# RWKV streams in three stages (front, inverse, chain), with TensorE's order written out in rounds

## The chip, the cores and the metric

One core of one Trainium2 chip runs the whole program in one launch. The metric is device time in microseconds, the median of several executions. The core has five engines with a queue each: TensorE (PE, matmuls and transposes; its weight loads are listed as PEld), VectorE (DVE), ScalarE (ACT), GpSimd (POOL) and SyncE (SP, which here issues the DMAs).

## The reference

Two layers of a hybrid backbone over 1024 latent tokens and 256 context tokens, width 1024. Layer 0 is RWKV-7 time mixing beside a Mamba-2 branch, layer 1 an mLSTM beside attention. The change touches only the RWKV branch, a delta rule that is run in both directions, first over the context and then, with the state left there, over the latent tokens:

```python
    def step(S, inp):
        r_t, k_t, v_t, w_t, a_t, kk_t = inp
        Skk = jnp.einsum('dbhvk,dbhk->dbhv', S, kk_t)
        S = S * w_t[..., None, :] - Skk[..., :, None] * (kk_t * a_t)[..., None, :] + v_t[..., :, None] * k_t[..., None, :]
        return S, jnp.einsum('dbhvk,dbhk->dbhv', S, r_t)
...
    w_pre = p['w0'] + jnp.einsum('btdr,drc->btdc', jnp.tanh(wl), p['w2'])
    decay = jnp.exp(-jnp.exp(-jax.nn.softplus(-w_pre) - 0.5))
    a = jax.nn.sigmoid(p['a0'] + jnp.einsum('btdr,drc->btdc', al, p['a2']))
    kk = hs(k * p['k_k'])
    kk = kk / jnp.maximum(jnp.sqrt(jnp.sum(kk * kk, -1, keepdims=True)), 1e-12)
    k_dir = k[:, :, None] * (1.0 + (a - 1.0) * p['k_a'])
    y, S_fin = rwkv7_bidir_scan(hs(r), hs(k_dir), hs(v), hs(decay), hs(a), kk, S0)
    # group norm of y per head, plus a bonus term, times the branch's gate
```

There are 8 heads of 64 columns: four blocks `ct` of 128 columns, two heads each. Everything is float32.

## The kernel before

The kernel cuts the 1280 tokens into chunks of 64 and works through them in closed form. A *unit* is two chunks (NG = 2) of one block of 128 columns in both directions, which makes four products `j` (two chunks, two directions) of two heads each; a block has NU = 10 units, the first two of them the context. Two streams run side by side: stream 0 does the blocks 0 and 1, stream 1 the blocks 2 and 3, 20 units each.

The parts, all generators whose `yield` marks the end of a step:

- `rwkv_prep(st, ct)`, once per block: five pieces of 256 tokens, four steps each. It loads r, k, v and the low-rank input `al` (single buffers, tags `pr`, `pk`, `pv`, `pal`), and in the same first step multiplies `al` with `a2`; then normalises kk (line 612 and following, with a square root on ScalarE and a reciprocal on VectorE), forms the bonus and turns v; results go to DRAM (`kk_d`, `bv_d`, `vt_d`).
- `rwkv_unit(st, ct, gi)`: first the *front*: loads of `wa`, r, k, kk and of v into SV, two matrix products into PSUM (tag `mm`), four tanh (line 686), the decay's running sum (`tensor_tensor_scan`), three exponentials, and the products AR, KB and RZ (lines 708 to 714). Then the *inverse*: the product MN (evacuated in line 730), transposes KT, MT and TT, and the inverse of a unit triangular matrix by doubling: an identity turn and five levels b = 2, 4, ..., 32. Each level has an X turn (evacuated by a masked multiplication into Xs, line 783), a T turn into Tm (lines 809, 816) and a TT turn into TT (line 817); a turn is 16 matmuls of 64x64 in two or four quadrants of the array. The PSUM tile `rec0` or `rec1` of a stream has one buffer of two banks, so a turn waits for the evacuation of the turn before.
- `rwkv_chain(st, ct, gi)`: the sequential part over the unit's two chunks: four short steps per chunk (pw, pu, pS, py) in the one-bank PSUM tile `ch0` or `ch1`, which carry the state in SV and write y (line 879).
- `rwkv_finish(st, ct)`, once per block: the norm over y, five turns and the gate (lines 887 to 916), which uses the tags `pr`, `pk`, `pv` of the preparation again.

`rwkv_stream` puts them in order. It runs `pace(unit q+1, chain q)`, which takes a step of the chain with every other step of the unit, and every third time a step of the side work (the next block's preparation from unit 4 on, the last block's finish). All side work goes through `alone`, a lock that one generator holds from its start to its end across both streams. At a block's unit 8 the stream stops until its side work is done; at a block's unit 0 it lets the unit run and holds the chain back while side work is left. `lockstep` takes one step of each stream in turn.

While the streams begin, `mix` puts in the part of the output projection that needs no RWKV result (`out_part`: two column halves, ten token tiles each, 24 matmuls per tile into PSUM `oa`, evacuated in line 1262), one step for `mix3` = 3.0 lock steps; when it is done the streams run on alone (`run(r)`). The rest of the projection (`out_gemm`) follows the streams.

The order of the instructions on each engine is made when the program is built: a planner takes the instruction that its own costs say is ready first, and the order in which the code issues them decides between several. Inside `tc.manual_schedule(engines={PE})` TensorE's instructions stay instead in the order in which the code issues them. The Mamba stage and the attention already stand in such a block; the RWKV stage does not. Every engine works its queue in that fixed order, and an instruction whose input is not there holds up what is behind it.

Of the kernel before, what the change touches and what calls it, by code (L numbers as in the profile page):

```python
# [149 lines left out]
class K:  # L150
    mix0 = 2.2
    mix2 = 1.25
    mix1 = 0.5
    mix3 = 3.0
    mixa = 0.6
# [396 lines left out]
    def rwkv_setup(s, rp):  # L552
# [18 lines left out]
        s.tt, s.wa, s.rz, s.mt = {}, {}, {}, {}  # L571
        for st in range(2):
            for i in range(2):
                s.tt[st, i] = rp.tile([128, 2 * NG, 64], F32, name=f"TT{st}{i}")
                s.wa[st, i] = rp.tile([128, 2, 2, 64 * NG], F32, name=f"wa{st}{i}")
                s.rz[st, i] = rp.tile([128, 2 * NG, 2, 64], F32, name=f"RZ{st}{i}")
                nc.gpsimd.memset(s.wa[st, i], 0.0)
                nc.gpsimd.memset(s.rz[st, i], 0.0)
            s.mt[st] = rp.tile([128, 2 * NG, 64], F32, name=f"MT{st}")
# [64 lines left out]

    def rwkv_unit(s, st, ct, gi):

# [15 lines left out]
        r, k, kk = tl("ur", [64]), tl("uk", [64]), tl("ukk", [64])  # L662
        par = s.tn[st] % 2
        s.tn[st] += 1
        wa = s.wa[st, par]
        TT, RZ, MT = s.tt[st, par], s.rz[st, par], s.mt[st]
        SV = X["sv", gi] = tl("SV", [2, 2, 64], 2)
        for d in range(2):
            for j in range(2):
                s.load(wa[H[d], j, d], s.u_rk[12 + j][H[d], sl[d]])  # L670
        for d in range(2):
            for x, src in ((r, s.u_rk[ct]), (k, s.u_rk[4 + ct]), (kk, s.kk_d[ct])):
                s.load(flat(x)[:, L * d:L * d + L], src[:, sl[d]])
        for d in range(2):
            vsrc = s.vt_d[ct][:, NG * gs[d]:NG * gs[d] + NG]
            for h in range(2):
                for q in range(2):
                    s.load(SV[H[1 - h], NG * d:NG * d + NG, q, h], vsrc[H[1 - h]])
        pp = s.psum("mm", (128, 2, 2, L))
        for j, w in ((0, s.w2), (1, s.a2)):  # L680
# [12 lines left out]
        for d in range(2):  # L693
# [4 lines left out]
            nc.vector.tensor_tensor_scan(v(P), sm[:, ::-1] if d else sm, v(sg), 0.0, ALU.mult, ALU.add)  # L698
        E2 = tl("E2", [64], 2)
        nc.vector.tensor_sub(sg, P, sg)  # L700
# [12 lines left out]
        for h in range(2):  # L713
            nc.gpsimd.tensor_mul(RZ[H[h], :, h], E2[H[h]], r[H[h]])

        def kb(j, h):

            return KB[H[h], j, 1 - h:3 - h].rearrange("p a b -> p (a b)")

        yield  # L720
        MN = tl("MN", [2, 2, 64], 2)
# [68 lines left out]

        Tm = tl("Tm", [64], 2)
        own = {(j, h): (h, j) for j in range(NJ) for h in range(2)}
# [5 lines left out]
        for n, b in enumerate((2, 4, 8, 16, 32)):  # L798
            px = pt_()
            iX = turn(MT, own, Tm, iT, side[n], area(px, 0), (lambda j: j // 2) if n else None)  # L800
            Xs = tl("Xs", [64])
            mask(Xs, area(px, 0), f"l{b}", n > 0)
            yield
            pz = pt_()
            if b < 32:
                iT = turn(TT, iTT, Xs, iX, (), area(pz, 0), (lambda j: j // 2) if n else None)
            if n == 0:
                Tm = tl("Tm", [64], 2)
                nc.scalar.copy(Tm.rearrange("p (b s) l -> p b (s l)", b=2), area(pz, 0))
                pt = pt_()  # L810
            else:
                pt = pz
            iTT = turn(Xs, iX, TT, iTT, side[n + 1], area(pt, 1), (lambda j: j % 2) if 0 < n < 4 else (lambda j: j // 2))
            if n and b < 32:
                Tm = tl("Tm", [64], 2)
                nc.scalar.copy(Tm.rearrange("p (b s) l -> p b (s l)", b=2), area(pz, 0))
            nc.scalar.copy(TT.rearrange("p (b s) l -> p b (s l)", b=2), area(pt, 1))
            yield
# [109 lines left out]
    def rwkv_stream(s, st, cts):  # L928

        seq = [(ct, gi) for ct in cts for gi in range(s.NU)]  # L930
        yield from s.alone(s.rwkv_prep(st, cts[0]))
        yield from s.rwkv_unit(st, *seq[0])
        side = []
# [3 lines left out]

        for q, (ct, gi) in enumerate(seq):
            if gi == 4 and ct != cts[-1]:
                side.append(s.alone(s.rwkv_prep(st, cts[cts.index(ct) + 1])))  # L940
            u = s.rwkv_unit(st, *seq[q + 1]) if q + 1 < len(seq) else iter(())
            while side and gi == 0:
                side = more()
                next(u, None)
                yield
            for i, _ in enumerate(pace(u, s.rwkv_chain(st, ct, gi))):
                if i % 3 == 2:
                    side = more()
                yield
            if gi == s.NU - 2:  # L950
                while side:
                    side = more()
                    yield
            if gi == s.NU - 1:
                side.append(s.alone(s.rwkv_finish(st, ct)))
        while side:
# [342 lines left out]
    def layer0(s):  # L1299
# [45 lines left out]
        oa = s.pool("oa")  # L1345
        mix(r, s.out_part(oa, 0, "wabo", range(4, 12), y0, range(10), s.xin, xa, "oa", 1, 1), s.mix3, lambda: True)
        oa.release()
        ob = s.pool("ob")
        s.load_gates(0, ob)
        W = s.out_weights(ob, ob, "wabo", range(4))  # L1350
        run(r)
        rp.release()
# [732 lines left out]
```

## Time and profile before

| | |
|---|---|
| median of 3 runs | 3806.43 us (3802.72 to 3806.52) |
| the profiled execution | 3797.94 us, span 3796.1 us |
| TensorE busy in the span | 3366.2 us (89%), 29178 matmuls |
| VectorE, ScalarE, GpSimd busy | 2208.6 (58%), 1493.0 (39%), 1116.6 us (29%) |
| mean granted TensorE clock | 0.92 |
| RWKV stage, 865 to 1925 us | 1060 us, TensorE busy 862.5, VectorE 616.2, ScalarE 482.6, clock 0.82 |

A row of the view by stretches gives the stretch and its length, then each engine's busy time with the number of its instructions (a query for one line or tile lists only the engines that it concerns), then the granted TensorE clock as a share of full speed, the share of the DMA engines' time, and GB/s. A row of the timeline gives start, duration, engine, line, operation, output and inputs by the program's tile names, tile shape, how many instructions were merged, and in brackets the engine's idle time before it with what ended it. Matmuls are pipelined and their ends are modelled, so a group's duration is longer than the time after which the next group may start.

### The profile page before, as it was taken

The page shows a single profiled execution, that of the slowest core. Times are in us where ns is not written, and L with a number is a line of the kernel's source. Part 1 is how long each engine was busy: PE and PEld are TensorE (multiplying, and loading weights), DVE is VectorE, ACT ScalarE, POOL GpSimd, SP SyncE. Part 2 cuts the span into 40 slices and gives each one's busy share as a digit, 9 for nine tenths or more (in the row PEclk, how much of TensorE's full clock was granted, in tenths as well). Part 3 has the DMA queues.
Part 4 walks back from the last instruction along what each step waited for, and adds up shares of the span by engine and source line. Part 5 has one row for each costly group of instructions (what it writes and reads, how often), then busy time and mean ns, then how long its engine had stood idle before and what let it go on. Part 6 is the DMA issues. An engine that isn't in the chain of part 4 may idle for free. (4 is left out here: it accounts for less than half of the span.)

```text
span 3796.1 us, 74040 instructions
## 1 busy us (share of the span) xinstructions
PE 3366.2 (89%) x29178; PEld 2650.6 (70%) x29178; DVE 2208.6 (58%) x4053; ACT 1493.0 (39%) x3219; POOL 1116.6 (29%) x1071
## 2 busy tenths in 40 slices
PE   7999998996888888789769899999999788999978
PEld 3687776773566666577557798788888566666757
DVE  3576487773566666466557705433443488777645
ACT  3232233333434545444433322322332225666751
POOL 0112276662333221222102112112222255444330
PEclk9999998896898978699779999999999899999989
DMA  6526444435543222221133332654554451000023
GB/s 237 180 75 199 137 166 155 157 124 181 149 127 98 69 71 67 75 56 47 36 106 101 120 95 85 190 180 139 161 163 143 138 165 53 23 23 22 19 81 111
DMA packets 394276, 429.58 MB, mean 113 GB/s; under 512 B 81376, under 2 KB 317760, under 8 KB 391368
## 3 DMA queue, kind: packets, MB, share of 16 engines
q1 hardware_dynamic: 393928, 424.83, 35.7%
q8 instruction: 231, 3.78, 0.4%
q14 instruction: 117, 0.96, 0.1%
HBM read 306.62 MB, written 118.05 MB: 112 GB/s over the span
## 5 line engine op out<-in xcount | busy, mean ns | idle before, releaser
L211 PE MATMUL mm<-hh,wh 128*128 128x512 f32 (+1 forms) x1640 | 634.7, 387 | 0.0
L211 PE MATMUL mm<-hh,wl 128*128 128x512 f32 (+1 forms) x1640 | 610.6, 372 | 0.6 <-POOL wl L358 0.6
L211 PE MATMUL mm<-hl,wh 128*128 128x512 f32 (+1 forms) x1640 | 608.7, 371 | 0.0
L358 POOL TENSOR_TENSOR wl<-wr,wh 128x1024 fp32r<-128x1024 f32 x99 | 249.3, 2522 | 544.2 <-ACT wh L357 500.7
L211 PEld LDWEIGHTS mm<-hh,wh 128*128 128x128 f32 x1640 | 315.0, 192 | 66.0 <-issue 12.2
L211 PEld LDWEIGHTS mm<-hl,wh 128*128 128x128 f32 x1640 | 314.2, 192 | 61.7 <-issue 10.4
L211 PEld LDWEIGHTS mm<-hh,wl 128*128 128x128 f32 x1640 | 313.5, 191 | 59.5 <-issue 3.4
L1830 POOL TENSOR_SCALAR aP<-aP,adn,one 128x1280 f32<-128x1280 f32 x128 | 192.5, 1504 | 282.0 <-DVE adn L1829 146.4
L211 PE MATMUL mm<-wh,hh 128*128 128x256 f32 x736 | 216.3, 294 | 0.0
L1823 DVE TENSOR_REDUCE amx<-sc 128x1 f32<-128x1024 f32 x128 | 156.0, 1219 | 100.5 <-PE sc L211 100.3
L211 PE MATMUL mm<-wl,hh 128*128 128x256 f32 x736 | 208.3, 283 | 2.7 <-POOL wl L358 1.8
L211 PE MATMUL mm<-wh,hl 128*128 128x256 f32 x736 | 207.6, 282 | 0.0
L214 PE MATMUL tp<-mk,aP 128*128 128x128 f32 x1280 | 181.0, 278 | 5.0 <-ACT aPT L1838 5.0
L1838 ACT COPY aPT<-tp 128x512 f32<-128x512 f32 x256 | 145.5, 588 | 80.6 <-PE tp L214 78.9
L211 PE MATMUL pv<-aPT,aV 128*64 128x256 f32 x1280 | 168.1, 393 | 0.0
L214 PEld LDWEIGHTS tp<-mk,aP 128*128 128x128 f32 x1280 | 142.5, 141 | 35.9 <-issue 20.4
L357 ACT CAST wh<-wr 128x1024 fp32r<-128x1024 f32 x99 | 103.3, 1046 | 154.4 <-PE mm L211 128.4
L211 PE MATMUL sc<-akT,aqs 128*128 128x512 f32 x512 | 153.3, 422 | 1.7 <-DVE aqs L1808 1.1
L1111 POOL TENSOR_SCALAR sel<-mk,mdfd,mdt 128x128 f32<-128x128 f32 x160 | 128.9, 821 | 74.3 <-DVE E L1135 56.7
L211 PE MATMUL oa<-wh,yh 128*128 128x512 f32 x288 | 128.7, 447 | 24.3 <-DVE o L1262 11.9
L783 DVE TENSOR_TENSOR Xs<-rec,mk 128x256 f32<-128x256 f32 x200 | 83.6, 422 | 103.7 <-PE rec L211 101.5
L211 PEld LDWEIGHTS mm<-wl,hh 128*128 128x128 f32 x736 | 139.9, 190 | 3.7 <-POOL wl L358 2.5
(423 smaller groups left out, 7881.3 us busy)
## 6 DMA issues: line engine op xcount, KB each, us to landing
wr<-in_wcd SPq DMA_DIRECT2D x60, 512.0 KB, 5.3
adaw<-in_ada SPq DMA_DIRECT2D x48, 512.0 KB, 5.2
R<-rowd SPq DMA_DIRECT2D x20, 1024.0 KB, 5.6
wr<-in_wab SPq DMA_DIRECT2D x38, 512.0 KB, 4.1
yr<-y SPq DMA_DIRECT2D x36, 512.0 KB, 3.7
xt<-xtok SPq DMA_DIRECT2D x20, 512.0 KB, 5.0
SV<-vtd SPq DMA_DIRECT2D x320, 32.0 KB, 2.2
lva<-lv SPq DMA_DIRECT2D x19, 514.0 KB, 5.5
```

What stands on the lines that cost most here:

```text
L211: return s.nc.tensor.matmul(out, lhsT, rhs, start=start, stop=stop)
L214: return s.nc.tensor.transpose(out, in_, ident)
L357: nc.scalar.copy(hi, raw)
L358: nc.gpsimd.tensor_sub(lo, raw, hi.bitcast(F32))
L783: nc.vector.tensor_mul(half(t), out.rearrange("p b (s l) -> p b s l", s=2), m_)
L1111: nc.gpsimd.tensor_scalar(sel[:, h], s.m("slt"), s.dfd[:, o:o + 1], dtb[:, h:h + 1], ALU.mult, ALU.add)
L1823: nc.vector.tensor_reduce(mx[:, 1:2], ps, AX.X, ALU.max)
L1830: nc.gpsimd.tensor_scalar(P, P, dn[:, 3:4], s.one, ALU.mult, ALU.mult)
L1838: copy(out, pp.rearrange("p (a b) q -> p a (b q)", a=out.shape[1]))
```

## The change

`rwkv_unit` is split: its front becomes the generator `rwkv_front`, which runs one unit further ahead, with its two products in PSUM tag `oa` in place of `mm`; what it hands on gets one more buffer (E2 and RZ three). SV's loads move to the start of the inverse. `rwkv_stream` runs rounds: in each, the inverse of unit q+1, the front of unit q+2 and the chain of unit q, a step of the inverse first, a lock step's end, then a step of the chain, in some iterations one of the front, in every other iteration one of the side work. Only the first preparation of each stream takes the lock. The next block's preparation starts at unit 1 (stream 0) or 4 (stream 1) and has to be done by unit 3 or 6; during a finish the chain of the next block's unit 0 is held back. Both loops of the stage stand in `manual_schedule` for TensorE, and `mix3` becomes 2.0. Tm gets one buffer for two, and there is one more yield inside the first level.

```diff
@@ class K
-    mix3 = 3.0
+    mix3 = 2.0
@@ rwkv_setup
         for st in range(2):
+            for i in range(3):
+                s.rz[st, i] = rp.tile([128, 2 * NG, 2, 64], F32, name=f"RZ{st}{i}")
+                nc.gpsimd.memset(s.rz[st, i], 0.0)
             for i in range(2):
...
-                s.rz[st, i] = rp.tile([128, 2 * NG, 2, 64], F32, name=f"RZ{st}{i}")
-                nc.gpsimd.memset(s.rz[st, i], 0.0)
@@
-    def rwkv_unit(s, st, ct, gi):
+    def rwkv_front(s, st, ct, gi):
...
-        par = s.tn[st] % 2
+        n = s.tn[st]
         s.tn[st] += 1
-        wa = s.wa[st, par]
-        TT, RZ, MT = s.tt[st, par], s.rz[st, par], s.mt[st]
-        SV = X["sv", gi] = tl("SV", [2, 2, 64], 2)
+        wa, RZ = s.wa[st, n % 2], s.rz[st, n % 3]
...
-        for d in range(2):
-            vsrc = s.vt_d[ct][:, NG * gs[d]:NG * gs[d] + NG]
-            for h in range(2):
-                for q in range(2):
-                    s.load(SV[H[1 - h], NG * d:NG * d + NG, q, h], vsrc[H[1 - h]])
-        pp = s.psum("mm", (128, 2, 2, L))
+        yield
+        pp = s.psum("oa", (128, 2, 2, L))
...
-        E2 = tl("E2", [64], 2)
+        E2 = tl("E2", [64], 3)
...
+        X["f", gi] = AR, KB, E2, RZ, n
+
+    def rwkv_unit(s, st, ct, gi):
...
+        AR, KB, E2, RZ, n = X.pop(("f", gi))
+        TT, MT = s.tt[st, n % 2], s.mt[st]
...
+        SV = X["sv", gi] = tl("SV", [2, 2, 64], 2)
+        for d in range(2):
+            g = NG * s.og(d, gi)
+            vsrc = s.vt_d[ct][:, g:g + NG]
+            for h in range(2):
+                for q in range(2):
+                    s.load(SV[H[1 - h], NG * d:NG * d + NG, q, h], vsrc[H[1 - h]])
...
-        yield
         MN = tl("MN", [2, 2, 64], 2)
...
-        Tm = tl("Tm", [64], 2)
+        Tm = tl("Tm", [64])
...
             if n == 0:
-                Tm = tl("Tm", [64], 2)
+                Tm = tl("Tm", [64])
                 nc.scalar.copy(Tm.rearrange("p (b s) l -> p b (s l)", b=2), area(pz, 0))
+                yield
                 pt = pt_()
@@ rwkv_stream
-        yield from s.alone(s.rwkv_prep(st, cts[0]))
-        yield from s.rwkv_unit(st, *seq[0])
...
-        for q, (ct, gi) in enumerate(seq):
-            if gi == 4 and ct != cts[-1]:
-                side.append(s.alone(s.rwkv_prep(st, cts[cts.index(ct) + 1])))
-            u = s.rwkv_unit(st, *seq[q + 1]) if q + 1 < len(seq) else iter(())
-            while side and gi == 0:
-                side = more()
-                next(u, None)
+        def part(fn, q):
+            return fn(st, *seq[q]) if 0 <= q < len(seq) else None
+
+        def step(g):
+            return g if g is not None and next(g, 0) is None else None
+
+        for _ in s.alone(s.rwkv_prep(st, cts[0])):
+            yield
+        for _ in s.rwkv_front(st, *seq[0]):
+            yield
+            yield
+        for q in range(-1, len(seq)):
+            gi = seq[q][1] if q >= 0 else -1
+            if q >= 0 and gi == 1 + 3 * st and seq[q][0] != cts[-1]:
+                side.append(s.rwkv_prep(st, cts[cts.index(seq[q][0]) + 1]))
+            u, f, c = part(s.rwkv_unit, q + 1), part(s.rwkv_front, q + 2), part(s.rwkv_chain, q)
+            i = 0
+            while u or f or c or (side and gi == 3 + 3 * st):
+                u = step(u)
                 yield
-            for i, _ in enumerate(pace(u, s.rwkv_chain(st, ct, gi))):
-                if i % 3 == 2:
+                if not (side and gi == 0):
+                    c = step(c)
+                if i % 2 == 0 and i != 2:
+                    f = step(f)
+                if i % 2 or gi == 0:
                     side = more()
+                i += 1
                 yield
-            if gi == s.NU - 2:
-                while side:
-                    side = more()
-                    yield
             if gi == s.NU - 1:
-                side.append(s.alone(s.rwkv_finish(st, ct)))
+                side.append(s.rwkv_finish(st, seq[q][0]))
@@ layer0
-        mix(r, s.out_part(oa, 0, "wabo", range(4, 12), y0, range(10), s.xin, xa, "oa", 1, 1), s.mix3, lambda: True)
+        with s.tc.manual_schedule(engines={mybir.EngineType.PE}):
+            mix(r, s.out_part(oa, 0, "wabo", range(4, 12), y0, range(10), s.xin, xa, "oa", 1, 1), s.mix3, lambda: True)
...
-        run(r)
+        with s.tc.manual_schedule(engines={mybir.EngineType.PE}):
+            run(r)
```

More of the change, by code (lines that the diff above doesn't have):

```diff
@@ L714, in rwkv_unit, with tl @@
             nc.gpsimd.tensor_mul(RZ[H[h], :, h], E2[H[h]], r[H[h]])
+        X["f", gi] = AR, KB, E2, RZ, n
+    def rwkv_unit(s, st, ct, gi):
+        nc, rp = s.nc, s.rp
+        X = s.RX[ct]
+        NJ = 2 * NG
+        H = [slice(0, 64), slice(64, 128)]
+        AR, KB, E2, RZ, n = X.pop(("f", gi))
+        TT, MT = s.tt[st, n % 2], s.mt[st]
+        def tl(nm, w, bufs=1):
+            return rp.tile([128, NJ] + list(w), F32, tag=f"{nm}{st}", name=s.name(nm), bufs=bufs)
+        SV = X["sv", gi] = tl("SV", [2, 2, 64], 2)
[5 more added lines that the diff above has]
+                    s.load(SV[H[1 - h], NG * d:NG * d + NG, q, h], vsrc[H[1 - h]])
         def kb(j, h):
             return KB[H[h], j, 1 - h:3 - h].rearrange("p a b -> p (a b)")
-        yield
         MN = tl("MN", [2, 2, 64], 2)
@@ L814, in rwkv_unit @@
             if n and b < 32:
-                Tm = tl("Tm", [64], 2)
+                Tm = tl("Tm", [64])
                 nc.scalar.copy(Tm.rearrange("p (b s) l -> p b (s l)", b=2), area(pz, 0))
```

## The prediction

> **What bounds the kernel now.** I read the page first, then busy time by stretches, then the counts of single source lines in the same stretches, then the timeline.
>
> ```profile
> span 3796.1 us, 74040 instructions
> PE   7999998996888888789769899999999788999978
> PEclk9999998896898978699779999999999899999989
> ```
>
> One slice is 94.9 us. The RWKV stage is slices 10 to 20; there TensorE's busy digit is 7 to 9 and its clock digit falls to 6, while slices 21 to 31 stand at 9 and 9. The stage runs from 865 us (first matmul of the output projection's part) to 1925 us (last store of the second finish):
>
> ```profile
> core 0: us, PE busy (x) PEld busy (x) DVE busy (x) ACT busy (x) POOL busy (x), PEclk, DMA share, GB/s
> 865.00:1045.00 180.00, 139.47 (x737) 88.76 (x737) 80.31 (x131) 74.29 (x130) 53.09 (x53) 0.76 0.55 166
> 1211.00:1495.00 284.00, 246.09 (x5190) 193.41 (x5190) 192.38 (x431) 153.77 (x433) 65.90 (x85) 0.84 0.26 70
> 1495.00:1621.00 126.00, 90.98 (x1502) 67.10 (x1498) 66.80 (x142) 57.68 (x149) 28.10 (x36) 0.69 0.25 72
> 1621.00:1852.00 231.00, 208.24 (x5145) 167.94 (x5146) 148.69 (x362) 109.64 (x361) 51.33 (x69) 0.95 0.18 46
> 1893.00:1925.00 32.00, 5.83 (x21) 3.19 (x22) 10.89 (x14) 8.58 (x15) 3.40 (x5) 0.50 0.26 78
> 865.00:1925.00 1060.00, 862.53 (x15296) 654.15 (x15297) 616.21 (x1286) 482.60 (x1291) 261.32 (x303) 0.82 0.31 88
> ```
>
> How many units fall in a stretch: line 730 evacuates a unit's first product in two instructions, one per head half.
>
> ```profile
> 1211.00:1495.00 284.00, 17.92 (x29) 0.84 0.26 70
> 1495.00:1621.00 126.00, 5.04 (x8) 0.69 0.25 72
> 1621.00:1852.00 231.00, 18.04 (x28) 0.95 0.18 46
> ```
>
> So a pair of units (one per stream) takes 231/7 = 33.0 us from 1621 on, where nothing else runs; 284/7 = 40.6 us in 1211 to 1495, beside the preparation of the next columns; and 1495 to 1621 brings only two pairs in 126 us, 60 us more than two undisturbed ones. In that last stretch stream 0's finish stands behind stream 1's preparation, since both take the lock of `alone`, and stream 0's chain stands behind its finish.
>
> Is TensorE full at 208 of 231 us? The timeline from 1774 us says no:
>
> ```profile
> 1774.28 0.46 PE L211 MATMUL rec<-Xs,TT 64*64 64x64 f32 x16 [0.57 <-DVE Xs L783]
> 1774.56 0.41 PE L211 MATMUL rec<-TT,Xs 64*64 64x64 f32 x16
> 1774.79 0.41 PE L211 MATMUL rec<-Tm,MT 64*64 64x64 f32 x16
> 1775.04 0.37 ACT L816 COPY Tm<-rec 128x256 f32<-128x256 f32 x1 [0.62 <-PE rec L211]
> 1775.27 0.42 DVE L783 TENSOR_TENSOR Xs<-rec,mk 128x256 f32<-128x256 f32 x1 [0.60 <-PE rec L211]
> 1775.31 0.38 ACT L817 COPY TT<-rec 128x256 f32<-128x256 f32 x1
> 1775.74 0.46 PE L211 MATMUL rec<-Tm,MT 64*64 64x64 f32 x16 [0.15 <-ACT TT L817]
> ```
>
> Sixteen matmuls are followed by the next sixteen 0.23 to 0.28 us later, though each group counts 0.41 to 0.46 us as busy. What bounds the stage is the loop matmul, evacuation, next matmul of the two streams, and the order in which their steps stand on TensorE.
>
> [...]
>
> **The change part by part.** *Front, inverse and chain in three units.* Before, a stream's unit is front then inverse in one generator; the chain of the unit before runs beside it. Now the front of the unit after next has its own place in each round. No operation of VectorE, ScalarE or TensorE is added; what goes is the front from the series. The inverse alone costs, by uncontended loops:
>
> ```profile
> 1794.62 0.94 PE L211 MATMUL rec<-AR,KB 64*128 64x128 f32 x12
> 1783.43 1.29 DVE L730 TENSOR_TENSOR MN<-rec,mk 128x512 f32<-128x512 f32 x2 [1.01 <-PE rec L211]
> 1784.86 0.47 PE L214 MATMUL rec<-mk,KB 64*128 64x64 f32 x8
> 1786.06 0.37 ACT L751 COPY KT<-rec 128x256 f32<-128x256 f32 x1
> 1789.26 0.68 PE L211 MATMUL rec<-Tm,MT 64*64 64x64 f32 x16
> 1789.99 0.43 DVE L783 TENSOR_TENSOR Xs<-rec,mk 128x256 f32<-128x256 f32 x1 [0.33 <-PE rec L211]
> 1790.60 0.68 PE L211 MATMUL rec<-Xs,TT 64*64 64x64 f32 x16
> 1719.66 0.70 PE L211 MATMUL mm<-wa,w 128*128 128x256 f32 x2 [0.29 <-ACT a L686]
> ```
>
> First product: about 1.1 (16 such matmuls) + 1.29 + 0.2 = 2.6 us. Transposes and their two copies: 1.2. The steps with two quadrants (identity turn, first X, first T): 1790.60 - 1789.26 = 1.34 each, and 1.2 for the fourth (its copy alone follows). Then three times X (1774.79 to 1775.69 and 0.1: 1.0) and T with TT (1774.28 to 1775.74: 1.46), and a last pair of 1.0 and 1.1. Sum 18.5 us in 14 steps, with a 15th call that ends the generator.
>
> *The fixed order.* In each of 15 iterations TensorE gets stream 0's inverse step, stream 1's, then chain, front and side work of each. The preparation's 20 yields of two streams, one after the other under the lock, put them about ten iterations apart, so step i meets step i+5 (modulo 15). The longer loop of each meeting, with 2.1 us where the front's four matmuls (two times 0.70) join, gives 2.6+1.2+1.5+1.3+2.1+1.2+1.5+1.5+1.1+1.5+2.6+1.5+1.3+1.3+2.1 = 24.3 us, the round's floor. To this come queues: VectorE works 148.69/7 = 21.2 us per pair and ScalarE 15.7, in a 30 us round 71% and 52%, so a result often waits for the rest of an instruction (148.69/362 = 0.41 us on VectorE): I take 0.4 us per iteration, 15 x 0.4 = 6. Round: 30 us. Its bounds are 25 (hardly any queue) and 40 (as with preparation beside it now).
>
> *The opening.* Projection tiles come every two lock steps, not three.
>
> ```profile
> 865.00:1045.00 180.00, 6.90 (x10) 0.76 0.55 166
> 865.00:1045.00 180.00, 5.94 (x10) 0.76 0.55 166
> 865.00:1925.00 1060.00, 148.42 (x479) 95.22 (x479) 13.82 (x20) 0.82 0.31 88
> ```
>
> The first row counts projection tiles (line 1262), the second preparations (line 612), the third is the projection's tile `oa` in the stage. Now 18 us pass per preparation of four steps, with one tile each. Two tiles each cost 24 x 148.42/479 = 7.4 us more, less the 40.5 us that TensorE idles in this stretch (180 - 139.47), 4 per preparation: 18 to 21.4, I take 19.5. Ten of these and four more steps: all 20 tiles are done at 865 + 200 = 1065, when stream 0 is half through its first inverse and stream 1 in its first front.
>
> *The locks removed, preparation spread.* Preparation starts in columns' unit 1 (stream 0) or 4 (stream 1), one step in two iterations; the finish runs ahead of the next columns' first chain, which moves back by two iterations. The 60 us of 1495 to 1621 go. Of preparation, what is left is its own cost: (40.6 - 33.0) x 7 = 53 us for the seven preparations that line 612 shows there:
>
> ```profile
> 1211.00:1495.00 284.00, 3.83 (x7) 0.84 0.26 70
> 1522.48 1.22 PE L211 MATMUL mm<-al,a 64*128 64x256 f32 x2 [3.23 <-DMA al<-urk]
> 1501.43 0.70 PE L211 MATMUL mm<-al,a 64*128 64x256 f32 x2 [1.83 <-DMA al<-urk]
> ```
>
> that is 7.6 each, with TensorE standing for the load of `al` behind it (1.83 and 3.23 us) and everything queued on it too. This stays, since load and matmul are still in one step: 10 x 7 = 70 us. The two finishes: 10 us.
>
> *Small edits.* A third RZ buffer per stream adds two memsets:
>
> ```profile
> L578 POOL MEMSET RZ<- x4: 526/526/527, 861.4 to 864.3; 128x512 f32 x4
> L178 SPq DMA_DIRECT2D SV<-vtd x320: 573/605/1637, 889.0 to 1850.4; - x160
> ```
>
> 1.1 us on POOL beside the first loads, nothing on the path. Tm with one buffer: its reader stands ahead of its writer on TensorE; nothing, or 0.4 us per round if not. The eight SV loads of a unit (0.605 us each on SP, 4.8) move to the start of the inverse, ahead of the front's ten loads. SV's buffer is free when the chain ends (iteration 8), the front's matmul is in iteration 4 of the next round, some 20 us on: covered; without that cover TensorE stands 2 to 3 us per stream and round. The front's matmuls share the projection's PSUM bank: one evacuation of 0.69 us (6.90/10) in the opening.
>
> **The sum**, in the profiled execution: 1065 + 20 rounds x 30 + 10 (last chain) + 70 + 10 + 32 (tail 1893 to 1925, unchanged) = 1787, for 1925: 138 us less. That execution took 3797.94 us (span 3796.1); the median of the three runs is 3806.43, 8.5 higher. Forecast: 3806 - 138 = 3668.
>
> **Rivals.** *The round gains nothing* (33 us as now): only the lull and the opening pay. 3668 + 20 x 3 = 3728. For it: in 1621 to 1852 TensorE's longest waits by the view of waits are already short (summed us, times, longest):
>
> ```profile
> PE rec L211 <- POOL AR L710: 8.1, 6, 1.6
> PE rec L211 <- ACT TT L817: 3.9, 14, 0.8
> PE rec L211 <- DVE Xs L783: 3.6, 7, 1.0
> ```
>
> Against: the first of them is the front in series, which the change takes off the path.
>
> *A denser round* (25 us, the floor): 3668 - 100 = 3568. For it: the clock, 0.95 undisturbed and 0.69 to 0.84 around, would rise with fewer gaps; against: VectorE would stand at 85%. [...]
>
> *Slower: the fixed order stands still.* TensorE waits at the head of its queue for one late evacuation, and the other stream's ready step, next chain and side work wait behind it. If 16 of VectorE's 21.2 us per pair fall into such waits on top of the 24.3, a round is 40 us, time 3668 + 200 = 3868. It decides at (1925 - 1187)/20 = 36.9 us per round. For it: the front gives VectorE long instructions (0.7 us and up) just between two evacuations. Against: they stand behind in program order. [...]
>
> *No change:* round 36.5 to 37.3.
>
> **Chances.** Forecast (27 to 32 us per round) 0.45; nothing in the round 0.20; denser 0.15; slower 0.15; none 0.05. Faster by over 0.2% (about what a measurement of this kernel tells from no change) 0.80, same 0.05, slower 0.15. The range takes in rounds of 25.4 to 35.8 us: 3575 to 3785.
>
> **What would show it.** Line 730's count in a window of 300 us without preparation: 20 or so if a round is 30 us, 18 at 33. Projection tiles all before some 1070 us. No stretch in which the clock falls to 0.69 for 126 us. The waits of `rec` matmuls for Xs and TT get more in number and stay under a microsecond; waits over 2 us for VectorE, or for `wa`, would prove the slower rival. The rest of the kernel keeps its time.

## The result and the profile after

The changed kernel takes 3820.64 us (median of 13 runs, 3809.51 to 3829.94) where the kernel before took 3798.67 beside it: a ratio of 1.006, 95% interval 1.0044 to 1.0077. It is slower by 0.6%; the forecast was 3668, faster by 3.6%. The profiled execution took 3812.7 us (span 3810.9).

The page of the changed kernel, first lines and the two TensorE lines in slices of 95 us:

```profile
span 3810.9 us, 74026 instructions
...
PE   7999998886678787677669899999999788999978
...
PEclk9999999997887888798779999999999899999989
```

Apart from one digit each in slices 8 and 9, TensorE's row differs only in slices 10 to 20: where it had stood mostly at 8 (6 to 9) it now stands at 6 to 8. The stretches of the changed kernel (columns as before: PE, PEld, DVE, ACT, POOL, granted clock, DMA share, GB/s):

```profile
865.00:1045.00 180.00, 124.50 (x445) 86.88 (x446) 69.75 (x93) 62.23 (x98) 56.71 (x51) 0.78 0.55 167
1204.00:1490.00 286.00, 222.26 (x5202) 180.51 (x5204) 184.31 (x429) 154.83 (x433) 65.90 (x86) 0.86 0.25 69
1490.00:1619.00 129.00, 89.58 (x2191) 73.34 (x2192) 83.92 (x181) 67.45 (x184) 32.94 (x40) 0.81 0.24 67
1619.00:1824.00 205.00, 162.00 (x4374) 136.27 (x4370) 128.45 (x313) 96.25 (x312) 47.48 (x60) 0.90 0.19 48
1853.00:1911.00 58.00, 26.36 (x590) 20.22 (x588) 23.19 (x43) 18.56 (x48) 3.62 (x5) 0.67 0.12 35
865.00:1937.00 1072.00, 777.60 (x15297) 617.04 (x15298) 605.75 (x1274) 486.83 (x1292) 263.12 (x302) 0.83 0.30 86
```

The evacuation of a unit's first product, which was line 730, is now line 746; its counts in the same stretches:

```profile
1204.00:1490.00 286.00, 18.05 (x29) 0.86 0.25 69
1490.00:1619.00 129.00, 7.69 (x12) 0.81 0.24 67
1619.00:1824.00 205.00, 15.42 (x24) 0.90 0.19 48
```

Twenty-four evacuations are six pairs of units: an undisturbed round takes 205/6 = 34.2 us, where it took 33.0 before and 30 was forecast. Seven pairs beside the preparation take 286/7 = 40.9 us (40.6 before). The stage is 1072 us long (1060 before), though TensorE's busy time in it fell from 862.5 to 777.6: the same matmuls fill fewer busy microseconds, and the rest became waiting.

Where the round waits, in a timeline of TensorE after 1645 us:

```profile
1646.16 0.46 PE L211 MATMUL rec<-Tm,MT 64*64 64x64 f32 x16
1648.21 0.71 PE L211 MATMUL rec<-TT,Xs 64*64 64x64 f32 x16 [1.59 <-DVE Xs L799]
1648.69 0.65 PE L211 MATMUL rec<-Xs,TT 64*64 64x64 f32 x16
1649.12 0.65 PE L211 MATMUL rec<-TT,Xs 64*64 64x64 f32 x16
1650.89 0.70 PE L211 MATMUL rec<-Tm,MT 64*64 64x64 f32 x16 [1.11 <-ACT TT L834]
1651.52 2.08 PE L211 MATMUL rec<-AR,KB 64*128 64x128 f32 x16
```

and of VectorE at the same time:

```profile
1645.30 0.42 DVE L704 SCALAR_TENSOR_TENSOR KB<-P,a 128x256 f32<-128x256 f32 x1
1646.34 1.36 DVE L707 TENSOR_TENSOR KB<-P,kd 64x256 f32<-64x256 f32 x2 [0.62 <-POOL kd L699]
1647.73 0.76 DVE L799 TENSOR_TENSOR Xs<-rec,mk 128x256 f32<-128x256 f32 x2
```

The X turn ends at about 1646.6, but its evacuation into Xs stands on VectorE behind the two KB halves of another unit's front, and these stand behind `kd` from GpSimd: 0.62 us of waiting and 1.36 of work. Xs begins at 1647.73, 1.1 us after its product is done, and TensorE waits 1.59 us. Right after that its matmuls take half as long again (0.71 and 0.65 for 0.46), and the next first product takes 2.08 us for 16 matmuls, where I had counted 1.1: from 1648 to 1654 us the granted clock is 0.50. VectorE's own waits, changed kernel 1619 to 1824 (summed us, times, longest):

```profile
DVE sg L684 <- ACT sg L681: 36.9, 12, 3.3
DVE Xs L799 <- PE rec L211: 18.6, 14, 3.2
DVE MN L746 <- PE rec L211: 8.2, 6, 1.6
```

and the kernel before, 1621 to 1852:

```profile
DVE Xs L783 <- PE rec L211: 36.3, 44, 2.1
...
DVE sg L689 <- ACT sg L686: 1.6, 1, 1.6
```

Before, VectorE idled for evacuations. Now it stands 12 times, once per unit, up to 3.3 us at the front's first instruction, because tanh is not done yet. In its rows above VectorE keeps to the order of its queue: the Xs of 1647.73, its product done at about 1646.6, comes after both KB halves.

### The profile page after: what moved, and what is told of

Its sections match the earlier page's. It is cut to its first block, busy times and chain, and to the rows that moved or that the text cites. A ratio compares the mean times of both kernels' runs of the same rounds, so it can differ in the third digit from the quotient of the medians.

```text
span 3810.9 us, 74026 instructions
## 1 busy us (share of the span) xinstructions
PE 3271.7 (86%) x29178; PEld 2607.2 (68%) x29178; DVE 2198.3 (58%) x4053; ACT 1497.6 (39%) x3221; POOL 1116.6 (29%) x1073
## 4 chain that ended last, share of the span: by engine, by line
PE 44%; DVE 13%; DMA 6%; issue 5%; ACT 4%; POOL 3%; SPq 1%; ACTq 0%; POOLq 0%; DVEq 0%
PE mm L211 19%; PE rec L211 5%; PE oa L211 4%; PE tp L214 4%; PE pv L211 4%; PE lm L211 3%; PE sc L211 3%; PE ch L211 2%; SPq L178 1%; DMA lkt<-lkt 1%; DVE MN L746 1%; PE sx L211 1%; DMA lRW<-lrow 1%; DMA wr<-in_wabo 1%; DVE MT L758 1%
## 5 line engine op out<-in xcount | busy, mean ns | idle before, releaser
L211 PE MATMUL oa<-wh,yh 128*128 128x512 f32 x288 | 127.7, 444 | 18.9 <-ACT wh L1265 10.7
L211 PEld LDWEIGHTS mm<-wh,hl 128*128 128x128 f32 x736 | 141.3, 192 | 1.2
```

What stands on the lines that cost most here:

```text
L211: return s.nc.tensor.matmul(out, lhsT, rhs, start=start, stop=stop)
```

## The experiments

All ratios are to the kernel before, on the same chip. Rounds are read from the evacuations of MN in the stretch where neither preparation nor finish runs.

**Who orders TensorE.** *new_planned*: both blocks of fixed order taken out of the changed kernel.

```diff
-        with s.tc.manual_schedule(engines={mybir.EngineType.PE}):
-            mix(r, s.out_part(...), s.mix3, lambda: True)
+        mix(r, s.out_part(...), s.mix3, lambda: True)
...
-        with s.tc.manual_schedule(engines={mybir.EngineType.PE}):
-            run(r)
+        run(r)
```

> The new streams with TensorE's order left to the planner (both blocks with the fixed order taken out). Theory A (the fixed order on TensorE is what costs: it adds to the opening and holds the round at 34 us): 3720 to 3760 us, the projection's tiles and the first units come as early as before, the round falls under 33 us. Theory B (the new streams themselves are no better: their iterations are bound by the loop matmul, evacuation, matmul and by VectorE's queue, whoever orders TensorE): 3790 to 3820, round 33 to 34 us.

3747.92 us, ratio 0.9877 (0.985 to 0.9905).

```profile
1574.00:1779.00 205.00, 173.45 (x4368) 143.30 (x4368) 130.75 (x313) 97.13 (x312) 47.75 (x60) 0.88 0.18 44
```

The pipeline alone gains 1.2%, and the fixed order costs 1.8%, more than that gain. But six rounds take 205 us here too: 34.2 us each, whoever orders TensorE. What differs is elsewhere: the 21st unit's MN comes at 1461 for 1500, and from the last MN to the chain's end it is 28 us for 53.

*old_fixed*: the same two blocks put around the loops of the kernel before, that is the new lines of the diff above on the old streams.

> The old streams with TensorE's order fixed in both loops of the stage, nothing else. Theory A: slower than before by 60 us or more (3860 and up), since the old order of steps was never laid out for it. Theory B: within 20 us of before (3780 to 3820), TensorE's order matters little.

3969.54 us, ratio 1.0459 (1.0434 to 1.0483), rounds of some 41 us. With the front in series the fixed order costs 171 us; with three stages about 73 (3820.64 against 3747.92).

*new_fixed_late*: the changed kernel with only the second loop (`run(r)`) fixed.

> The changed kernel, but the opening (streams mixed with the projection's part) planned and only the loop after it fixed. If the fixed order is what makes the opening late (the tenth unit 45 us later than before), that comes back: 3770 to 3785. If the opening is late by the new places of the parts (two tiles per preparation, front ahead), it stays at 3810 to 3825.

3808.72 us, ratio 1.0027 (1.0007 to 1.0046). The tiles end at 1109 for 1115 and the first MN comes at 1005 for 1021, but by the 30th MN that lead is gone, and the profiled stages end within 1 us of each other. The median is 12 us lower, and the intervals of the two ratios just overlap. So the opening's order is worth 12 of the 73 us at most, and even these are not certain.

**The lull.** *old_prep_early*: the kernel before, with the next block's preparation begun where the change begins it.

```diff
-            if gi == 4 and ct != cts[-1]:
+            if gi == 1 + 3 * st and ct != cts[-1]:
```

> The kernel before with one number changed: stream 0 starts its second preparation at unit 1 and not 4, so that it has let the lock go before stream 1's starts and stream 0's finish doesn't wait for the lock. If the 60 us lost in 1495 to 1621 are the lock's: 3740 to 3765 us. If they are the finish's own work and the held-back chain: 3785 to 3800.

3793.41 us, ratio 0.9991 (0.9972 to 1.0009): nothing. The preparations' last store came 45 us earlier (1490 for 1535), but the finish's first turn only 8 us earlier (1530 for 1538), the thin stretch spread over others, and the stage ended at 1926 us (1925 before). In the changed kernel 1490 to 1619 holds three pairs in 129 us: 26 us more than three of its undisturbed rounds, where the kernel before lost 60.

**The finish at the head of TensorE's queue.** The end of the stage on TensorE, changed kernel:

```profile
1870.89 0.46 PE L211 MATMUL rec<-TT,Xs 64*64 64x64 f32 x16 [1.30 <-DVE Xs L799]
1879.21 1.06 PE L214 MATMUL mm<-mk,y 128*64 128x128 f32 x4 [7.85 <-DVE y L918]
1881.49 1.06 PE L214 MATMUL mm<-mk,y 128*64 128x128 f32 x4 [1.22 <-ACT yt L930]
1885.94 1.06 PE L214 MATMUL mm<-mk,y 128*64 128x128 f32 x4 [3.39 <-ACT yt L930]
1890.48 1.06 PE L214 MATMUL mm<-mk,y 128*64 128x128 f32 x4 [3.48 <-ACT yt L930]
1891.47 0.70 PE L211 MATMUL ch<-SV,MN 128*64 128x64 f32 x8
```

These are four of the five finish transposes of stream 0. Each needs the one PSUM buffer `mm`, which ScalarE empties into the one `yt`, and stream 1's last chain (`ch`) stands behind them for 20 us. *fixed_finish_free* gives the finish two places, in PSUM and for its three tiles:

```diff
-            pp = s.psum("mm", (128, 4, 128))
+            pp = s.psum("oa" if g % 8 else "mm", (128, 4, 128))
...
-            gt = rp.tile([128, 256], F32, tag="pr", name=s.name("gt"))
+            gt = rp.tile([128, 256], F32, tag="psm" if g % 8 else "pr", name=s.name("gt"))
```

(and `bv`, `yt` likewise with `pkk` and `pa1`).

> The changed kernel; the finish alternates between two PSUM banks and two sets of its three buffers, so that its transposes no longer wait for the piece before to be stored. If the finish's transposes at the head of TensorE's queue hold up the other stream's chain (20.3 us of waits for yt in 1204 to 1600, and 35 us for a chain's last steps in 1871 to 1906): 3780 to 3800 us, the last chain ends 15 us or more earlier. If the end is only the length of the last chain: 3810 to 3825.

3795.77 us, ratio 0.9985 (0.9964 to 1.0006), 25 us under the changed kernel. TensorE's wait in the last stretch, first of the changed kernel and then of this one:

```profile
PE mm L214 <- ACT yt L930: 24.0, 8, 4.4
PE mm L214 <- DVE y L918: 17.9, 2, 10.1
```

```profile
PE mm L214 <- DVE y L918: 17.9, 2, 10.1
PE mm L214 <- ACT yt L930: 4.6, 4, 2.3
```

The last chain now ends 42 us after the last MN, where it took 53: 11 us less, not the 15 that I expected. The same wait stands in the middle finish (20.3 us from 1204 to 1600) and is gone there too. So the finish's single places, PSUM and tiles together, are shown to cost the changed kernel 25 us. Not all of that is the fixed order's: the waits for `yt` stand in new_planned as well (37.1 us from 1118 on, 44.3 in the changed kernel), and below the same edit helps a planned kernel by 11 us.

**VectorE's queue.** *fixed_kb_twice* issues the KB halves of line 707 twice; *fixed_kb_pool* gives them to GpSimd.

```diff
             nc.vector.tensor_mul(KB[H[h], :, 2 - 2 * h], P[H[h]], kd[H[h]])
+            nc.vector.tensor_mul(KB[H[h], :, 2 - 2 * h], P[H[h]], kd[H[h]])
```

```diff
-            nc.vector.tensor_mul(KB[H[h], :, 2 - 2 * h], P[H[h]], kd[H[h]])
+            nc.gpsimd.tensor_mul(KB[H[h], :, 2 - 2 * h], P[H[h]], kd[H[h]])
```

> The changed kernel with the front's two half-width multiplications into KB written twice, about 1.4 us more VectorE work per unit and nothing else. Theory V (the round is 34 us because the front's VectorE work now stands in one queue with the evacuations of the inverse): the round grows by 2 to 3.5 us, 3870 to 3900. Theory L (the round is bound by the loops matmul, evacuation, matmul, with VectorE 62% busy beside them): the round stays at 34, 3815 to 3830.

> The changed kernel with the same two multiplications on GpSimd in place of VectorE: 1.4 us less on VectorE per unit, 1.6 more on GpSimd. Theory V: the round falls to 31 to 32.5 us, 3760 to 3790. Theory L: no change, 3815 to 3830. If GpSimd's work slows VectorE's own instructions: 3830 or more.

Twice: 3832.32 us, ratio 1.0098 (1.0065 to 1.0131), round 217/6 = 36.2 us. On GpSimd: 3804.20, ratio 1.0015 (0.9996 to 1.0034), round 191/6 = 31.8. The round moved by +2.0 and -2.4 as foretold; the totals moved by 12 and -16 us only, since the seven rounds beside the preparation changed by less (291/7 = 41.6 and 278/7 = 39.7 us for 40.9). The totals expected were missed, the round's mechanism held. In the undisturbed rounds VectorE's and ScalarE's other instructions stand in the same order in all three kernels, so nothing but the halves was moved there.

*planned_kb_pool* puts the second edit on new_planned.

> The changed kernel with both TensorE orders left to the planner, and the two KB half multiplications (line 707) on GpSimd. Theory V (what the front gives VectorE to do stands in front of the evacuations, whoever orders TensorE): the round 1574 to 1779 falls from 34.2 us by about 2.4, as it did under the fixed order, and the time from 3748 to 3725-3738. Rival (the planner has already put the front's multiplications where they delay nothing, so that its 34.2 us have another cause): the round stays within 0.5 us of 34.2 and the time within 3740-3755.

3713.62 us, ratio 0.9782 (0.9753 to 0.9811). Its undisturbed rounds, whole and MN alone:

```profile
1563.00:1735.00 172.00, 150.85 (x4374) 124.52 (x4372) 118.86 (x290) 97.58 (x312) 66.20 (x84) 1.00 0.22 55
```

```profile
1563.00:1735.00 172.00, 15.46 (x24) 1.00 0.22 55
```

172/6 = 28.7 us per round, 5.5 less, twice what I expected. VectorE lost 11.9 us of work in six rounds (130.75 to 118.86), yet 33 us went. TensorE's busy time for the same matmuls fell by 22.6 us (173.45 to 150.85), with the granted clock at 1.00 for 0.88, and its longest wait fell from 1.6 to 0.9 us. In new_planned the halves stood in front of the evacuation of MN:

```profile
1641.65 1.81 DVE L707 TENSOR_TENSOR KB<-P,kd 64x256 f32<-64x256 f32 x2
1643.49 1.29 DVE L746 TENSOR_TENSOR MN<-rec,mk 128x512 f32<-128x512 f32 x2
1644.83 0.46 PE L214 MATMUL rec<-mk,KB 64*128 64x64 f32 x8 [1.61 <-DVE MN L746]
```

I read this so: a wait of 1.6 us costs itself and the slow matmuls behind it (0.71 and 0.65 us for 0.46 after the wait of 1.59 us in the changed kernel). But the planner also put some of the other instructions in a different order here, unlike in the fixed pair above, so it is not shown how much of the 5.5 us is due to the halves alone.

**TensorE's series.** *fixed_first_twice* issues each matmul of the first product twice.

```diff
-                s.mm(pa[h][:, j]..., kb(j, h), AR[H[h], j]...)
+                for _ in range(2):
+                    s.mm(pa[h][:, j]..., kb(j, h), AR[H[h], j]...)
```

> The changed kernel with each of the 16 matmuls of a unit's first product (AR, KB) issued twice into the same place. In 1619-1824 their first issue is busy 19.6 us for 12 units, 1.63 us a unit, 3.3 us a round. If a round is the series of what TensorE has to do and its waits (the queue in fixed order has no free place): the round grows by 3 to 4 us, from 34.2 to 37.5, and the time by 25 to 60 us. Rival (TensorE idles 43 of these 205 us while evacuations run, and more matmuls fall into that; VectorE is what decides): the round grows by under 1 us and the time by under 10 us.

3900.82 us, ratio 1.026 (1.023 to 1.029), 80 us above the changed kernel: past the end of what I expected.

```profile
1673.00:1906.00 233.00, 182.25 (x4567) 157.84 (x4568) 132.39 (x314) 96.39 (x312) 50.17 (x60) 0.86 0.17 42
```

233/6 = 38.8 us per round, 4.6 more for 3.3 us of matmuls. TensorE idles 43 of 205 us, and nothing of this fell into the idle time. The first product runs at half clock in part: its single matmuls take 0.271 to 0.578 us, and 32 of them 3.94 us soon after a wait of 1.60 for Xs. In the changed kernel 16 take 1.16 us at 1694.87, with the granted clock at 1.00, and the 2.08 us of 1651.52 at 0.50.

*one_by_one* runs the streams one after the other:

```diff
-        r = lockstep([s.rwkv_stream(0, (0, 1)), s.rwkv_stream(1, (2, 3))])
+        r = lockstep([g for g in [chain(s.rwkv_stream(0, (0, 1)), s.rwkv_stream(1, (2, 3)))]])
```

> The changed kernel with the second stream started when the first has ended, so that a round holds one stream's inverse, front and chain. It measures the loops by themselves: by the prediction's sum 18.5 us and a small queue, 19 to 21 us a round. If a lone round takes 24 us or more, the floor of 24.3 us that the prediction gave to two streams was too low (theory L), whatever VectorE does.

One run, 4211.31 us. Its lone rounds:

```profile
1437.00:1614.00 177.00, 124.24 (x2560) 101.44 (x2556) 76.28 (x184) 57.40 (x182) 32.01 (x35) 0.70 0.12 31
```

Seven rounds in 177 us: 25.3 us for one stream with no other to meet. That is more than the 24.3 us that I had put as the floor for two.

**Both helpful edits together.** *fixed_free_pool* is the changed kernel with the finish's two places and the KB halves on GpSimd, *planned_free_pool* the same with TensorE planned (no new lines of code).

> The changed kernel, fixed order, with both edits that helped it: finish on two pools (-28 us alone) and KB halves on GpSimd (-17 us alone). If they act at different places (end and middle stretch; rounds), they add: 3770-3782, ratio 0.991-0.995, and still 25-35 us above new_planned: what is left is the fixed order's cost in places other than the finish. Rival (both shorten the same wait, the queue of stream 1's last chain): 3793-3803.

> The same with the finish's transposes and products alternating between two PSUM pools and two sets of buffers. If the finish stands in the way only where TensorE's order is fixed, this adds nothing to planned_kb_pool but a few us in the last finish (46 us from the chain's end to the last store in new_planned): 0 to -12 us against it, so 3713-3738. Rival (the finish also costs the planned order some 28 us): 3700-3710.

3772.19 us, ratio 0.9929 (0.9903 to 0.9954), and 3702.22, ratio 0.9745 (0.9716 to 0.9775). In the fixed order the two add: 48 us together, 25 and 16 alone. In the planned order the finish's places are worth 11 us more than planned_kb_pool, inside the rival's range: the finish costs that order too. With the halves on GpSimd the places gain 32 us in fixed order (3804.20 to 3772.19) and 11 planned, so only some 21 us of the finish belong to the order. The gap between the two orders is still 70 us. It builds up all along: the first MN is 20 us later in fixed order, the 21st 42, the 39th 62, the last store 73.

**The opening.** TensorE's longest wait from 865 to 1118 in the changed kernel is the preparation's first product, which stands for its load:

```profile
PE mm L211 <- DMA al<-urk: 31.4, 6, 15.0
```

Six kernels tried to shorten it. *fixed_prep_ahead* and *planned_free_pool_ahead* put a step between that load and its product; *fixed_mix3* and *planned_free_pool_mix3* go back to `mix3 = 3.0`:

```diff
             s.load(al, s.u_rk[13][:, sl])
+            yield
             sm = t_("sm")
```

```diff
-    mix3 = 2.0
+    mix3 = 3.0
```

> The changed kernel with one more yield in each preparation, between its loads and its first products, so that in TensorE's fixed order a step of the other stream or of the tiles stands between them. If the opening's missing 50 us come from the fixed order's product standing first in the queue for a load of al (31.4 us of waits in 865-1118, 8 more in 1204-1490), the last tile ends at 1085 to 1100 for 1115 and the time falls by 15 to 35 us, to 3785-3805. Rival (the opening is bound by the transfers and the tiles' evacuations; a fifth step only makes each preparation longer): the last tile within 8 us of 1115 and the time 3810-3850.

> planned_free_pool with the extra yield in the preparations. There the waits for al are 11.5 us in the opening and 12.8 us in 1115-1465. If these are on the path: 3680-3698. Rival (the planner already works beside them): 3698-3708.

> The changed kernel with mix3 back at 3.0, the one number of the opening that the change moved: a step of the tiles after every third step of the streams in place of every second. If the denser mixing is what made each of the first ten preparations 22.8 us long (870 to 1098), the preparations end some 20 us earlier, the first MN too, the last tile 20 to 40 us later, and the time moves by under 10 us or falls by up to 20. Rival (the tiles are the bound of the opening and what they are delayed by is lost at the end): the time grows by 10 to 30 us.

> planned_free_pool with mix3 at 3.0. A planner that orders TensorE itself should mind the mixing less than the fixed order does: within 10 us of 3702. Rival (the mixing also sets the planner's order of buffers, so that it moves the opening as under the fixed order): 10 to 30 us off it.

fixed_prep_ahead: 3806.68 us, ratio 1.0019 (0.9999 to 1.0039), last tile at 1121. Its median is 14 us lower, but not by the opening: waits for `al` fell to 23.0 us, and those for the tiles' weights rose from 10.7 to 22.5. Its profiled execution (3815.53 us) does not show where the 14 us went. planned_free_pool_ahead: 3712.66, ratio 0.9772 (0.974 to 0.9804), 10 us worse than without. fixed_mix3: 3842.82, ratio 1.0115 (1.0075 to 1.0154): preparations end earlier (the eleventh begins at 1070 for 1098), tiles end at 1159, waits for `al` grow to 55.3 us, and the whole is 22 us slower. planned_free_pool_mix3: 3695.59, ratio 0.9726 (0.9694 to 0.9757), the lowest time of this study, though its interval overlaps that of planned_free_pool.

The runs show what the mixing costs a preparation. From one load of `al` to the next, the first nine steps take 19.0 us in the kernel before, 23.3 in the changed one and 20.1 with `mix3` back at 3.0; planned_free_pool has 22.2, and 18.1 with `mix3` = 3.0. The denser mixing makes a preparation 3.2 to 4.1 us longer, whoever orders TensorE. Most of it falls into two of the nine steps, 34 and 33 us long in the changed kernel, each with a column half's first tile. This is the first:

```profile
883.44 0.43 SPq L178 DMA_DIRECT2D al<-urk  x1
916.17 0.32 SPq L181 DMA_DIRECT2D kkd<-kk  x1
917.01 0.44 SPq L178 DMA_DIRECT2D al<-urk  x1
```

From 883 to 918 TensorE stands 7.0 us for the tile's weights. The other steps take 17 to 24 us.

*fixed_few_loads* loads the tiles' input `yr` once in each column half (the other tiles then compute from the first one's), and *fixed_store_pool* issues the tiles' stores from GpSimd:

```diff
-                yr = t("yr", [kt, 128], yb)
-                s.load(yr, y[:, ks[0]:ks[0] + kt, ts])
+                if not few:
+                    yr = t("yr", [kt, 128], yb)
+                    s.load(yr, y[:, ks[0]:ks[0] + kt, ts])
```

```diff
-                s.store(dst[i][:, cs], x)
+                (nc.sync if l else nc.gpsimd).dma_start(dst[i][:, cs], x)
```

> The changed kernel with the tiles' yr (512 KB, 18 loads between 865 and 1118, 9.4 MB of the 40.0 MB that move there) loaded only once in each half; the other tiles use the first one's, so their values are not the reference's, and all else is as before. If the transfers are what the opening waits for, the waits of TensorE for al fall from 31.4 us to under 16, the last tile ends at 1075 to 1095 and the time falls by 15 to 40 us. Rival (the steps of a preparation, one engine after the other, and the tiles between them; the loads land late only because SP issues them late, behind loads that wait for a buffer): the last tile within 10 us of 1115, the waits for al over 20 us, the time within 12 us of 3820.

> The changed kernel with the 20 stores of the opening's tiles (xa<-x) issued by GpSimd, whose addition they follow, in place of SP. In SP's list of 918-983 each store of a tile stands in front of v, yr, x, the store of kk and al of the next preparation (933.25 xa, 936.45 kkd, 936.82 al; 950.45, 953.65, 954.31; 969.52, 972.49, 972.99), and one such turn takes 17 to 19 us, about as long as a preparation. If this queue is what sets the opening's step, al is issued earlier, TensorE's waits for al fall from 31.4 us to under 16, the last tile ends at 1080-1100 and the time falls by 15 to 35 us. Rival (the store of kk, which ends a preparation's own series of steps, holds al just as well; or TensorE and the evacuations set the step): the last tile within 10 us of 1115 and the time 3808-3835.

3823.95 us, ratio 1.0051 (1.0035 to 1.0067), and 3819.40, ratio 1.0076 (1.0046 to 1.0106); the last tile at 1121 and 1119, the waits for `al` 27.0 and 34.6 us. Neither these bytes (30.9 MB for 40.0 in the stretch) nor the tiles' stores in SP's queue are the cause. What stayed the same in fixed_store_pool is this pair on SP, here 18 us apart:

```profile
940.26 0.38 SPq L181 DMA_DIRECT2D kkd<-kk  x1
940.69 0.42 SPq L178 DMA_DIRECT2D al<-urk  x1
...
958.15 0.38 SPq L181 DMA_DIRECT2D kkd<-kk  x1
958.59 0.42 SPq L178 DMA_DIRECT2D al<-urk  x1
```

A preparation's `al` is loaded right after the kk of the one before is stored, and kk is formed from the single buffer of `al`. So a preparation's whole series (load, products, tanh, root, reciprocal) would repeat with nothing overlapped, and that would set the 17 us or more of every step, before the change as after it. A second `al` buffer would tell; it was not tried, and this is argued only.

## Why the prediction was wrong

From 865 us the forecast's sum was 1065 + 600 + 122 = 1787. Measured: 1115 + 20 x 34.2 + 138 = 1937. So 50 us are the opening, 84 the rounds, 16 the rest. The rest is a remainder, in which errors both ways meet: the lull and the tail below cost more than forecast, while the seven preparations beside the rounds cost 6.7 us each (40.9 less 34.2), where ten had been put at 7.

- **The queue allowance of 0.4 us per iteration** (the step *The fixed order*) failed, and with it the round of 30 us. I priced VectorE's load as half an instruction in front of each evacuation. But the front, taken off the series, brings whole runs of instructions: the KB halves with their wait for GpSimd delay one evacuation by about a microsecond. Adding and removing those halves moved the round by +2.0 and -2.4 us, which shows that cause for 2.4 of the 4.2 us that the round is too long. For the other 1.8 the cause stays open. The longer waits of VectorE for tanh (36.9 us in six rounds) were seen only in the trace; no run took them away, and new_planned has half of them (19.4 us) in a round of the same length. The same step put the fixed order itself, beside the planner's, at no cost: it costs 73 us, and without it the change would have gained 1.2%.
- **The floor of 24.3 us**, from uncontended loops at full clock, was too low: a lone stream takes 25.3. I had left out the chain and the front between the loops, and the clock, which was 0.70 in those rounds, with TensorE busy for 124.24 of 177 us. The first product was counted at full clock (1.1 us) and takes up to 2.08.
- **The round of 30 us is possible**: 28.7 with the KB halves on GpSimd and TensorE planned. That is less than the 29.7 us per round for which TensorE was busy before (208.24/7): busy time itself fell, with the granted clock at 1.00 for 0.95, to 150.85/6 = 25.1 us per round.
- **The opening** (19.5 us per preparation, tiles done at 1065): the preparations came 870 to 1098, 22.8 us each, and the tiles ended at 1115, at 1109 and 1112 with TensorE planned there. That is above even my upper end of 21.4. TensorE's idle time, of which I meant to fill 4 us per preparation, grew: it was 40.5 us in 180 before and is 66 in the 233 from 865 to 1098. Two terms were too small. The 18 us per preparation came from ten rows in 180 us, but ten rows are nine steps, and from load to load these take 19.0. And the denser mixing, put at 1.5 us (19.5 less 18), costs 3.2 in fixed order and 4.1 planned, which the runs with `mix3` = 3.0 show. The loads of `yr` and the tiles' stores are ruled out; why even the shortest steps take 17 us is argued only.
- **The 60 us of the lull** went in part: 26 are left (three pairs in 129 us). The lock was not what cost them, as the prediction read it: with the preparations early the kernel before gained nothing.
- **The tail**, put in the sum as unchanged, grew: from the last MN to the last store it was 73 us before (1852 to 1925) and is 84 (1853 to 1937), since the last chain now stands behind the finish's transposes (53 us from the last MN to the chain's end for 41 before). With two places for the finish it is 65 us.
- **The slower rival** had the mechanism in part. TensorE did stand at the head of its queue, but not in the undisturbed rounds, where no wait for VectorE passed 1.6 us and planning TensorE changed nothing; over the whole stage waits for Xs and MN reach 3.6 and 4.3 us, past the 2 us that the prediction named as a sign. It stood in the finish (7.85 us and four times 1.2 to 4.4 with the chain behind it) and in the opening (up to 15.0). And the sign turned far below the point of 36.9 us per round that I gave, because that point assumed the 1065.
- **The small edits**: TensorE's waits from 1118 to 1937 name neither `wa` nor SV's loads nor RZ's memsets. The shared PSUM bank, put at 0.69 us in the opening, costs two waits there, 3.6 us together.
- **A sign misread**: for a window of 300 us the prediction gave a count of line 730 of 20 or 18. These are units; the line runs twice per unit, so the counts would be 40 and 36.

Of the 73 us that the fixed order costs, runs of their own give the finish some 21 and the opening 12 at most. Beside new_planned the changed kernel is 16 us late at the first MN, 39 at the 21st, 56 at the last and 65 at the last store: the cost is spread over the stage, and no single cause was found.

## What to carry to other kernels

Work taken off a series still stands in some engine's queue (here the KB halves, with Xs behind them 1.1 us late): list what it will stand in front of there, with the waits that it brings along, before calling it free. A fixed order on one engine should be tried apart from the restructuring that it came with; here the restructuring gained 1.2% and the order lost 1.8%. Before writing an order by hand, look for steps that need a single buffer (here the finish's PSUM place and its three tiles, behind which the last chain stood for 20 us).

## What the runs showed of the hardware

TensorE's clock fell to half after short waits. In the rounds of the changed kernel no wait of TensorE is longer than 1.6 us, yet the granted clock is 0.90, and the timeline shows half speed right after waits of 1.59 and 1.11 us. The clock drops to 0.50 seven times between 1619 and 1824 us, for 3.4 or 6.8 us each. In a stretch before each drop as long as the shortest of them, 3.4 us, TensorE was busy for 1.2 to 1.9 us and idle for 1.5 to 2.3, with no idle stretch above 1.6 us.

With the KB halves on GpSimd under the planner the clock went from 0.88 to 1.00 and six rounds from 205 to 172 us.

The KB halves, two VectorE multiplications, took 0.84 us as a pair at 1703 us, when GpSimd was idle, and 1.36 and 1.37 us beside GpSimd's AR multiplication at 1646 and 1714. In the kernel before a pair took 1.81 us at 1657, beside GpSimd's RZ and AR multiplications, and in new_planned 1.81 at 1641. On GpSimd a half took 0.73 us (medians of 0.725 in planned_kb_pool and 0.727 in fixed_kb_pool). At 1646 the pair took 0.52 us longer than at 1703, and GpSimd's instruction of 0.72 us had 0.65 us left to run when it began. Why the pair takes longer there is not shown.
